# First pass of a two-layer encoder kernel: normalisation folded into the transposes, the conditioning row spread from eight columns, and a new order around the first strips

## The chip, the cores and the metric

The kernel runs on one core of one Trainium2 chip. The metric is device time in microseconds (us) for one execution of the whole kernel. The engines are named as the profile names them: PE (TensorE matmuls), PEld (its weight loads), DVE (VectorE), ACT (ScalarE), POOL (GpSimd) and SP (the queue that issues the DMAs).

## The reference, cut to what matters

A sequence of 1024 tokens of width 1024 goes through two layers, differential attention and latent attention, each with a modulated RMSNorm ahead of it. The changed part is the head of layer 0: the modulation from c, the normalised and modulated h, and the first projections of h.

```python
def _rmsnorm(x, g):
    y = xf * lax.rsqrt(jnp.mean(xf * xf, axis=-1, keepdims=True) + RMS_EPS)
    return (y * g).astype(x.dtype)

def _modulation(c, ada_w, ada_b):
    mod = jax.nn.silu(c) @ ada_w + ada_b
    shift, scale, gate = jnp.split(mod[:, None, :], 3, axis=-1)

for i in range(DEPTH):
    shift, scale, gate = _modulation(c, ada_w[i], ada_b[i])
    h = _rmsnorm(x, norm_g[i]) * (1.0 + scale) + shift
    ...            # layer 0: proj = h @ w_in0; q, k, v, z; differential attention; w_out0
    x = x + gate * y
return _rmsnorm(x, final_norm_g)
```

## The kernel before, in words

**Layout.** h is kept transposed: eight chunks k of 128 features by 512 tokens, for each half of the tokens. Every projection is summed over the eight chunks in PSUM. To keep f32 accuracy at the rate of the fp32r type, each operand is split into a high part (an fp32r cast on ACT) and a low part (the difference, on POOL or DVE), and each product is three matmuls: high by high, high by low, low by high.

**Modulation.** `mod_dot` (line 439) is one DVE instruction over 128x1024: it multiplies a block of `ada` weights, 128 output features by 1024, by silu(c) spread over all partitions, and sums along the row. A chunk needs two of them, shift into `modb` and scale into `moda`; line 447 then makes `moda` = (1 + scale) * norm_g. The spread row lies in the PSUM bank `cb`: c is loaded as one row (`crow`, line 565), goes through tanh on ACT and a product on DVE (lines 600 and 601), and two matmuls with a row of ones spread it (line 605).

**First half of the first pass** (lines 670 to 718, the loop over k from -1). For each chunk: two `ada` loads of 512 KB and a `w_v0` load, the two dots, four transposes of 128x128 of the x tiles into the bank `tr` (`h_chunk`, line 487), the two ACT readings of that bank (line 492 the high part, line 494 the f32 value), and on POOL the low part (line 497). x has been scaled by 1/rms before: the first 256 columns of each tile on ACT (lines 618 and 621), the rest on DVE (line 624, `x_rest`). Then PE sums four value tiles (`vacc`, lines 712, 713, 717) and the first key strip (`kacc`, lines 714, 715, 718), 15 matmuls of 128x512 for a chunk. Ahead of the pass PE runs matmuls of ones by ones (`keep_busy`, line 561; `WARM` gives their number before and after the spread of c).

**Between the halves.** The first query strip `wq0` is cast and split (line 218 on ACT, 219 on DVE), the x tiles of the second half are squared and scaled, `strip_half` sums the query strip for the first half in a bank of the tag `acc` (24 matmuls), and `store_v` (lines 377 and 378) evicts the four `vacc` banks.

**Second half of the first pass** (lines 739 to 755). The same chunks for the other 512 tokens, with 96 matmuls into four `vacc` banks; `tr` and a half of `cb` take the transposes in turn. Four dots of layer 1 (`mods_g`) stand between these chunks. After it come the second half of the key and query strips, and from there on a long run of matmuls to the end.

**Order.** The program text gives dependences; a scheduler at compile time orders the instructions on each engine. `tc.issue_after(ins)` puts what its block emits behind `ins` on the engine of `ins`. Buffers of a tag rotate: `ada` has four, `tr` one, `cb` one, `acc` two and `accx` three banks.

Of the kernel before, what the change touches and what calls it, by code (L numbers as in the profile page):

```python
# [11 lines left out]
F32 = mybir.dt.float32  # L12
# [9 lines left out]
P = 128  # L22
# [9 lines left out]
_W = [("norm_g0", KT), ("ada_bsh0", KT), ("ada_bsc0", KT), ("norm_g1", KT), ("ada_bsh1", KT),  # L32
      ("ada_bsc1", KT), ("subln_g", 1), ("q_a_norm_g", 3), ("kv_a_norm_g", 2), ("inv", 1), ("ada_bg0", KT), ("ada_bg1", KT)]
VEC, NVEC = {}, 0
# [27 lines left out]
X_ACT0 = (0, 2)  # L62
X_CUT = 256
WARM = (8, 9)
SIN_AT = (4, 5, 7)
# [16 lines left out]
def trunk(ctx: ExitStack, tc: tile.TileContext, A, out):  # L82
# [292 lines left out]
    def store_v(l, sp, acc, tt, fh, tag="vst", bufs=None):  # L375
        v = sp.tile([P, 2, HF], F32R, name="v_hl", tag=tag, bufs=bufs or VB[l])
        store_v.act = S.copy(v[:, 0, :], acc).ins
        V.tensor_sub(v[:, 1, :], acc, f32v(v[:, 0, :]))
# [62 lines left out]
    def mod_pair(l, j, ws, c_):  # L441

        g, bsh, bsc, a_, b_ = mods[l]
# [3 lines left out]
        return V.scalar_tensor_tensor(out=a_[:, js], in0=a_[:, js], scalar=1.0, in1=g[:, js], op0=ALU.add, op1=ALU.mult).ins  # L447

# [28 lines left out]

    def h_chunk(l, xn4, k, dst, hp, sub=G, wide=False, act=False, f32=None):

        _, _, _, a_, b_ = mods[l]  # L480
        if wide:
            tr = bank("cb", "trc", [P, D])[:, :HF].rearrange("p (j q) -> p j q", j=4)
        else:
            tr = bank("tr", "trh", [P, 4, P])
        for j in range(len(xn4)):
            nk = KT // len(xn4[j])
            PE.transpose(tr[:, j, :], xn4[j][k // nk][:, (k % nk) * P : (k % nk + 1) * P], ident)
# [4 lines left out]
        h_chunk.act = S.activation(hh, tr[:, :n, :], AF.Identity, bias=bk, scale=ak).ins  # L492
        if act:
            h_chunk.act = S.activation(tmp, tr[:, :n, :], AF.Identity, bias=bk, scale=ak).ins
        else:
            V.tensor_scalar(tmp, tr[:, :n, :], ak, bk, op0=ALU.mult, op1=ALU.add)
        return sub.tensor_sub(hl, tmp, f32v(hh)).ins
# [64 lines left out]

    crow = p1.tile([P, D], F32, name="crow", tag="ada", bufs=ADA_B)
    th = p1.tile([P, D], F32, name="cth", tag="ada", bufs=ADA_B)
    SP.dma_start(crow[0:1, :], A["c"])
    xs0 = [load_x(0, 0)]
# [32 lines left out]

    c_act = S.activation(th[0:1, :], crow[0:1, :], AF.Tanh, scale=0.5).ins  # L600
    c_last = V.scalar_tensor_tensor(out=crow[0:1, :], in0=th[0:1, :], scalar=1.0, in1=crow[0:1, :], op0=ALU.add, op1=ALU.mult).ins
    cb = bank("cb", "cb", [P, D])
    for f in range(2):
        fs = slice(f * HF, f * HF + HF)
# [5 lines left out]
    y0 = [None] * 4  # L610
    ss0 = sm.tile([P, 4], F32, name="xss")
# [4 lines left out]
    for j in range(3):  # L616
        y0[j] = y_[:, j : j + 1]
        S.mul(xs0[j][0][:, :X_CUT], xs0[j][0][:, :X_CUT], y0[j])
    sq_halves([xs0[3][0][:, :HF], xs0[3][0][:, HF:]], ss0[:, 3:4])
    y0[3] = inv_rms(ss0[:, 3:4], 1)[:, 0:1]  # L620
    h_chunk.act = S.mul(xs0[3][0][:, :X_CUT], xs0[3][0][:, :X_CUT], y0[3]).ins

    def x_rest(j):
        V.tensor_scalar(xs0[j][0][:, X_CUT:], xs0[j][0][:, X_CUT:], y0[j], None, op0=ALU.mult)

# [4 lines left out]
    def sines(n):  # L630
        with tc.issue_after(h_chunk.act):
            if n == 0:
                S.activation(kk, ang, AF.Sin, scale=0.5)
                S.activation(nsin, ang, AF.Sin, scale=-1.0)
            if n == 1:
                S.activation(ang, ang, AF.Sin)
                S.copy(c2, cb)
# [23 lines left out]
    for k in range(-1, KT + SKEW):  # L661
        if k + 1 < KT:
# [15 lines left out]
        if k < 0:  # L678
            with tc.issue_after(m_last):
                x_rest(0)  # L680
                x_rest(1)
        if k == 0:
            with tc.issue_after(m_last):
                x_rest(2)
                x_rest(3)
        if k == X1_AT:
            with tc.issue_after(mod_load.last):
                qraw = fetch_strip([A["w_s0"][0, 0, f] for f in range(2)], [4, 4])
            with tc.issue_after(fetch_strip.last):
                xs1 = [load_x(1, j) for j in range(4)]  # L690
            x_last = load_x.last
            with tc.issue_after(h_chunk.act):
                wq0 = split_strip(qraw, None, ada_pair)
            q_split = load_strip.last
        if 0 <= k < KT:
            h_chunk(0, xs0, k, h0[k][0], p1, act=True)
            if k % 4 == 0:
# [21 lines left out]
    ssa, ssb = [sm.tile([P, 2], F32, name="xss") for _ in range(2)]  # L719
    with tc.issue_after(m_last):  # L720
        for j in range(2):
            sq_piece(xs1[j][0], ssa[:, j : j + 1], False)
    with tc.issue_after(h_chunk.act):
        for j in range(2):
            sx = sm.tile([P, 1], F32, name="xs2")
            sq_piece(xs1[2 + j][0], ssb[:, j : j + 1], True)
            sq_piece(xs1[2 + j][1], sx, True)
            V.tensor_add(ssb[:, j : j + 1], ssb[:, j : j + 1], sx)
    norm_x(ssa, xs1[:2])
    yb = inv_rms(ssb, 2)  # L730
    for j in range(2):
        V.tensor_scalar(xs1[2 + j][0], xs1[2 + j][0], yb[:, j : j + 1], None, op0=ALU.mult)
        S.mul(xs1[2 + j][1], xs1[2 + j][1], yb[:, j : j + 1])
    load_tables()

    qacc = strip_half(wq0, h0, 0)
    q_mm = mm3.last
    for tt in range(4):
        store_v(0, p1b, vacc[tt], tt, 0)
    vacc = [bank("acc", "vacc") for _ in range(4)]  # L740
    for k in range(KT + SKEW1):
        if k < KT:
            if 0 < k <= MODS_K:
                next(mods_g)
            with tc.issue_after(q_split), tc.issue_after(q_mm):
                h_last = h_chunk(0, xs1, k, h0[k][1], p1, V if k in HL_V else G, k % 2 == 1)
        if k >= SKEW1:
# [69 lines left out]
    for h in range(NH):  # L817
        items += [(strip0(1, h), h0, k_done(h)), (strip0(0, h), h0, q_done(h)), (strip0(2, h), h0, z_done(h))]
    wv1 = [load_wv(A["w_v0"][k, 1], V) for k in range(WV1)]
    with tc.issue_after(mod_load.last):  # L820
        z0raw = fetch_strip([A["w_s0"][2, 0, f] for f in range(2)], [4, 4])
    with tc.issue_after(store_v.act):
        wv1 += [load_wv(A["w_v0"][k, 1], V) for k in range(WV1, KT)]
# [19 lines left out]
    for i in range(2):  # L843
        V.tensor_mul(lam4[:, 2 * i, :], lam4[:, 2 * i, :], lam4[:, 2 * i + 1, :])
        V.reduce_sum(lp[:, i : i + 1], lam4[:, 2 * i, :], axis=AX.X)
# [1586 lines left out]
def layout(inputs):  # L2432
# [40 lines left out]
    small["q_a_norm_g"] = cols(I["q_a_norm_g"], 3)  # L2473
    small["kv_a_norm_g"] = cols(I["kv_a_norm_g"], 2)
    small["inv"] = ca(np.tile(_ROPE_INV, 4).reshape(P, 1))
    w = I["w_in1"]
# [28 lines left out]
```

## Time and profile before

| | |
|---|---|
| median of 3 runs | 1382.29 us (1381.32 to 1382.38) |
| the profiled execution, its own time | 1382.89 us |
| its span | 1380.9 us |
| PE busy | 1361.0 us, 99% of the span |
| DVE, ACT, POOL busy | 949.2, 738.3, 708.7 us |
| first matmul of the first pass starts | 14.94 us |
| last matmul of the second half of the pass starts | 81.75 us |

Times inside the trace are counted from the start of the span. A busy PE is not PE at its peak: a matmul is shown with its latency (0.39 us for 128x512) though the next one starts sooner, so the spacing of the starts is read instead. The granted clock (PEclk) is the share of full TensorE speed.

### The profile page before, as it was taken

How to read it: one execution, taken by the hardware profiler on the slowest of the kernel's cores; microseconds unless marked ns; L12 is line 12 of the kernel's file. 1: busy time of each engine (PE TensorE's matmuls, PEld its weight loads, DVE VectorE, ACT ScalarE, POOL GpSimd, SP SyncE). 2: the span in 40 equal slices, each digit the busy share in tenths (PEclk: the TensorE clock that was granted, in tenths of full speed). 3: DMA queues.
4: the chain of work that ended last, by engine and by line, in shares of the span. 5: the costliest groups of instructions: out<-in, count | busy, mean ns of one | idle time of the engine just before them, and what ended most of it. 6: DMA issues, size and time to landing. Idle time of an engine off the chain costs nothing.

```text
span 1380.9 us, 20717 instructions
## 1 busy us (share of the span) xinstructions
PE 1361.0 (99%) x7322; PEld 1144.8 (83%) x7322; DVE 949.2 (69%) x1334; ACT 738.3 (53%) x1357; POOL 708.7 (51%) x556
## 2 busy tenths in 40 slices
PE   8999999999999999999999999999999999999997
PEld 6788888888888888887887887788888888888886
DVE  7764788877777767778597987645566555555584
ACT  5633465565655656566648543345454454455554
POOL 4425163647585757565695135532141373834673
PEclk8999999999999999999999999999999999999999
DMA  9867644353444444526654255599343463576373
GB/s 335 275 177 222 211 108 143 113 146 103 156 114 149 135 122 130 153 71 204 210 202 170 60 160 183 161 284 286 115 117 111 111 214 123 190 222 229 118 264 122
DMA packets 149386, 232.06 MB, mean 168 GB/s; under 512 B 20641, under 2 KB 57633, under 8 KB 149282
## 3 DMA queue, kind: packets, MB, share of 16 engines
q1 hardware_dynamic: 149138, 230.48, 53.4%
q8 instruction: 57, 0.93, 0.3%
q14 instruction: 47, 0.39, 0.1%
q10 hardware_dynamic: 144, 0.26, 0.1%
HBM read 144.74 MB, written 61.81 MB: 150 GB/s over the span
## 4 chain that ended last, share of the span: by engine, by line
PE 88%; DVE 4%; DMA 2%; ACT 2%; issue 1%; POOL 1%; SPq 0%; POOLq 0%; DVEq 0%; ACTq 0%
PE s L2109 10%; PE acc L173 9%; PE acc L175 9%; PE acc L174 9%; PE tr L398 8%; PE s L869 8%; PE pv L173 4%; PE pv L174 4%; PE pv L175 4%; PE oy L173 2%; PE oy L174 2%; PE oy L175 2%; PE vps L173 2%; PE vps L174 2%; PE vps L175 2%; PE zacc L175 1%
## 5 line engine op out<-in xcount | busy, mean ns | idle before, releaser
L400 ACT CAST pth<-tr 128x512 fp32r<-128x512 f32 x256 | 150.2, 587 | 279.2 <-PE tr L398 276.3
L401 DVE TENSOR_TENSOR ptl<-tr,pth 128x512 fp32r<-128x512 f32 x256 | 176.3, 689 | 144.6 <-ACT pth L400 143.9
L415 DVE TENSOR_REDUCE nm<-s 128x1 f32<-128x1024 f32 x192 | 234.0, 1219 | 53.7 <-PE s L869 42.9
L219 POOL TENSOR_TENSOR wl<-wraw,wh 128x512 fp32r<-128x512 f32 (+2 forms) x73 | 93.4, 1280 | 264.4 <-ACT wh L218 185.8
L417 ACT ACTIVATE e<-s,nm 128x1024 f32<-128x1024 f32 x128 | 143.7, 1122 | 35.0 <-DVE nm L415 34.4
L398 PE MATMUL tr<-ident,e 128*128 128x128 f32 x1024 | 154.8, 273 | 1.8 <-DVE ptl L401 1.5
L398 PEld LDWEIGHTS tr<-ident,e 128*128 128x128 f32 x1024 | 121.3, 140 | 42.5 <-DVE ptl L401 19.7
L173 PE MATMUL acc<-h0h,wh 128*128 128x512 f32 x360 | 149.5, 415 | 0.0
L173 PE MATMUL pv<-pth,vt 128*128 128x256 f32 x512 | 147.6, 288 | 0.0
L174 PE MATMUL pv<-ptl,vt 128*128 128x256 f32 x512 | 145.4, 284 | 0.0
L175 PE MATMUL pv<-pth,vt 128*128 128x256 f32 x512 | 144.6, 282 | 0.0
L175 PE MATMUL acc<-h0h,wl 128*128 128x512 f32 x360 | 142.0, 394 | 0.0
L174 PE MATMUL acc<-h0l,wh 128*128 128x512 f32 x360 | 141.4, 393 | 0.0
L174 PEld LDWEIGHTS pv<-ptl,vt 128*128 128x128 f32 x512 | 97.5, 190 | 2.5
L1203 POOL TENSOR_TENSOR wol<-wol,woh 128x512 fp32r<-128x512 f32 x56 | 81.9, 1486 | 34.0 <-ACT woh L1202 31.8
L173 PEld LDWEIGHTS pv<-pth,vt 128*128 128x128 f32 x512 | 97.2, 190 | 2.5
L175 PEld LDWEIGHTS pv<-pth,vt 128*128 128x128 f32 x512 | 97.4, 190 | 0.0
L869 PE MATMUL s<-ks,qa 128*128 128x512 f32 x256 | 82.7, 402 | 1.3 <-DVE e L877 1.2
L877 DVE SCALAR_TENSOR_TENSOR e<-s,z,e 128x1024 f32<-128x1024 f32 x64 | 82.2, 1284 | 2.2
L175 PEld LDWEIGHTS acc<-h0h,wl 128*128 128x128 f32 x360 | 67.6, 188 | 14.7
L869 PE MATMUL s<-ks,qb 128*128 128x512 f32 x256 | 79.6, 392 | 0.0
L174 PEld LDWEIGHTS acc<-h0l,wh 128*128 128x128 f32 x360 | 68.2, 189 | 9.2
(433 smaller groups left out, 3416.8 us busy)
## 6 DMA issues: line engine op xcount, KB each, us to landing
ada<-in_ada_ss SPq DMA_DIRECT2D x32, 512.0 KB, 6.1
vS<-v_hl SPq DMA_DIRECT2D x32, 512.0 KB, 5.5
vt<-vS SPq DMA_DIRECT2D x32, 512.0 KB, 4.6
wraw<-in_w_s SPq DMA_DIRECT2D x60, 256.0 KB, 2.8
wol<-tS SPq DMA_DIRECT2D x56, 256.0 KB, 5.3
tS<-ob SPq DMA_DIRECT2D x48, 256.0 KB, 2.2
rp_sw<-rp_raw SPq DMA_DIRECT2D x160, 64.0 KB, 2.0
bc_s<-bc_d SPq DMA_DIRECT2D x34, 256.0 KB, 4.0
```

The source lines that it names most:

```text
L173: PE.matmul(psum, ah, bh, start=first, stop=False, skip_group_check=skip)
L174: PE.matmul(psum, ah, bl, start=False, stop=False, skip_group_check=skip)
L175: mm3.last = PE.matmul(psum, al, bh, start=False, stop=last, skip_group_check=skip).ins
L219: sub = (V if pair_of else G).tensor_sub(l_[:, :n], raw[:, :n], f32v(h_[:, :n]))
L398: transpose_p.last = PE.transpose(tr[:, j, :], p[:, kt * P : (kt + 1) * P], ident).ins
L400: mk["S"] = S.copy(pth[kh][:, :, dst], tr).ins
L401: mk["V"] = V.tensor_sub(ptl[kh][:, :, dst], tr, f32v(pth[kh][:, :, dst])).ins
L415: mk["V"] = V.reduce_max(nm, s_ps, axis=AX.X, negate=True).ins
L417: mk["S"] = S.activation(e, s_ps, AF.Exp, bias=nm, scale=1.0, accum_out=zs).ins
L869: PE.matmul(s_ps[:, kc * HF : (kc + 1) * HF], src[:, c, ql], KS[h][kc][:, c, :], start=fst, stop=not fst)
L877: combined.append(V.scalar_tensor_tensor(out=e0, in0=e1, scalar=z1[:, 0:1], in1=e0, op0=ALU.mult, op1=ALU.add).ins)
L2109: PE.matmul(s_ps[:, kc * HF : (kc + 1) * HF], lhs, rhs(kc), start=i == 0, stop=i == 4)
```

## The change

What it does, part by part:

- `h_chunk` takes a diagonal matrix `dg`. In the first pass x is no longer scaled: the transpose by the identity becomes an ordinary f32 matmul of the x tile by diag(1/rms). `dg0` is built by four ACT products of 128x128, `dg1` (second half) by four on DVE. `x_rest` and the scaling of the second half's x go.
- c comes with the small vectors, as eight columns of 128. tanh and product run over 128x8; eight DVE products make diag(c_k), and eight f32 matmuls of ones by diag(c_k) spread it in `cb`.
- The matmuls of ones after the spread go from 9 to 15, and three more of them stand behind the first chunk's transposes (`KEEP0`).
- (1 + scale) * norm_g moves from DVE (line 447) to an ACT instruction of 128x1 (`mod_scale`).
- The copy of `cb` to `c2` and the casts of `wq0` move behind the last chunk of the first half on ACT. The first query strip is summed in the second half of the `cb` bank, and not in an `acc` bank.
- `store_v` of the first half is put behind the squares on ACT and the diagonals on DVE, the second half's ACT readings behind `store_v`; the four layer-1 dots go behind the last chunk; some casts of the later strips, the first `w_v0` casts for the other features (two early ones and not three) and the products for lambda are put behind named instructions.

```diff
-WARM = (8, 9)
+WARM = (8, 15)
+KEEP0 = 3
-    def strip_half(w, rhs, half):
+    def strip_half(w, rhs, half, acc=None):
-        acc = bank("acc", "acc")
+        acc = bank("acc", "acc") if acc is None else acc
...
-        mod_dot(ws[1], bsc[:, js], a_[:, js], c_)
-        return V.scalar_tensor_tensor(out=a_[:, js], in0=a_[:, js], scalar=1.0, in1=g[:, js], op0=ALU.add, op1=ALU.mult).ins
+        return mod_dot(ws[1], bsc[:, js], a_[:, js], c_).ins
+    def mod_scale(l, j):
+        S.activation(a_[:, js], a_[:, js], AF.Identity, bias=g[:, js], scale=g[:, js])
...
-            PE.transpose(tr[:, j, :], xn4[j][k // nk][:, ...], ident)
+            if dg is None:
+                PE.transpose(tr[:, j, :], piece, ident)
+            else:
+                h_chunk.tr = PE.matmul(tr[:, j, :], piece, dg[:, j, :], start=True, stop=True).ins
...
-    SP.dma_start(crow[0:1, :], A["c"])
-    c_act = S.activation(th[0:1, :], crow[0:1, :], AF.Tanh, scale=0.5).ins
-    c_last = V.scalar_tensor_tensor(out=crow[0:1, :], ...).ins
-        spread = PE.matmul(cb[:, fs], ones[0:1, :], crow[0:1, fs], start=True, stop=True).ins
+    c_act = S.activation(th, part("c"), AF.Tanh, scale=0.5).ins
+    V.scalar_tensor_tensor(out=cs, in0=th, scalar=1.0, in1=part("c"), op0=ALU.add, op1=ALU.mult)
+    for k in range(KT):
+        c_last = V.tensor_scalar(cd[:, k, :], ident, cs[:, k : k + 1], None, op0=ALU.mult).ins
+        spread = PE.matmul(cb[:, k * P : k * P + P], ones, cd[:, k, :], start=True, stop=True).ins
...
-        S.mul(xs0[j][0][:, :X_CUT], xs0[j][0][:, :X_CUT], y0[j])
+        diag(dg0[:, j, :], y_[:, j : j + 1])          # S.mul(dst, ident, y)
...
-                S.copy(c2, cb)                         # in sines(1)
-            with tc.issue_after(h_chunk.act):          # at k == X1_AT
-                wq0 = split_strip(qraw, None, ada_pair)
-            h_chunk(0, xs0, k, h0[k][0], p1, act=True)
+            mod_scale(0, k)
+            h_chunk(0, xs0, k, h0[k][0], p1, act=True, dg=dg0)
+            if k == 0:
+                with tc.issue_after(h_chunk.tr):
+                    for _ in range(KEEP0):
+                        PE.matmul(kacc[:, 0:P], ones, ones, start=True, stop=True)
...
+    with tc.issue_after(h_chunk.act):                  # after the first half's loop
+        S.copy(c2, cb)
+        wq0 = split_strip(qraw, None, ada_pair)
-    norm_x(ssa, xs1[:2])
-    ...                                                # scaling of xs1[2:] on DVE and ACT
+    diags(0, inv_rms(ssa, 2))
+    dg_last = diags(2, inv_rms(ssb, 2))
-    qacc = strip_half(wq0, h0, 0)
+    cbq = bank("cb", "cbq", [P, D])
+    qacc = strip_half(wq0, h0, 0, cbq[:, HF:])
+    turn += 1
     for tt in range(4):
-        store_v(0, p1b, vacc[tt], tt, 0)
+        with tc.issue_after(x_last), tc.issue_after(dg_last):
+            store_v(0, p1b, vacc[tt], tt, 0)
...
-            if 0 < k <= MODS_K:
-                next(mods_g)
-            with tc.issue_after(q_split), tc.issue_after(q_mm):
-                h_last = h_chunk(0, xs1, k, ..., k % 2 == 1)
+            with tc.issue_after(store_v.act), tc.issue_after(q_mm):
+                h_last = h_chunk(0, xs1, k, ..., cbq if k % 2 else None, dg=dg1)
+        if k == KT:
+            with tc.issue_after(h_chunk.v):
+                for _ in range(MODS_K):
+                    next(mods_g)
...
-    wv1 = [load_wv(A["w_v0"][k, 1], V) for k in range(WV1)]
+    with tc.issue_after(h_chunk.act):
+        wv1 = [load_wv(A["w_v0"][k, 1], V) for k in range(2)]
...
-    wz0 = split_strip(z0raw)
+    with tc.issue_after(store_v.act):
+        wz0 = split_strip(z0raw)
```

More of the change, by code (lines that the diff above doesn't have):

```diff
@@ L62 @@
 X_ACT0 = (0, 2)
-X_CUT = 256
-WARM = (8, 9)
+WARM = (8, 15)
+KEEP0 = 3
 SIN_AT = (4, 5, 7)
@@ L377, in store_v @@
         store_v.act = S.copy(v[:, 0, :], acc).ins
-        V.tensor_sub(v[:, 1, :], acc, f32v(v[:, 0, :]))
+        store_v.v = V.tensor_sub(v[:, 1, :], acc, f32v(v[:, 0, :])).ins
         th, tl = tt // 4, tt % 4
@@ L476, in norm_x, with h_chunk @@
                     V.tensor_scalar(piece, piece, y[:, j : j + 1], None, op0=ALU.mult)
-    def h_chunk(l, xn4, k, dst, hp, sub=G, wide=False, act=False, f32=None):
+    def h_chunk(l, xn4, k, dst, hp, sub=G, wide=None, act=False, f32=None, dg=None):
         _, _, _, a_, b_ = mods[l]
-        if wide:
-            tr = bank("cb", "trc", [P, D])[:, :HF].rearrange("p (j q) -> p j q", j=4)
+        if wide is not None:
+            tr = wide[:, :HF].rearrange("p (j q) -> p j q", j=4)
         else:
@@ L486, in h_chunk @@
             nk = KT // len(xn4[j])
-            PE.transpose(tr[:, j, :], xn4[j][k // nk][:, (k % nk) * P : (k % nk + 1) * P], ident)
+            piece = xn4[j][k // nk][:, (k % nk) * P : (k % nk + 1) * P]
+            if dg is None:
+                PE.transpose(tr[:, j, :], piece, ident)
+            else:
+                h_chunk.tr = PE.matmul(tr[:, j, :], piece, dg[:, j, :], start=True, stop=True).ins
         n = len(xn4)
@@ L561, in keep_busy @@
             PE.matmul(warm[:, 0:P], ones, ones, start=True, stop=True)
-    crow = p1.tile([P, D], F32, name="crow", tag="ada", bufs=ADA_B)
-    th = p1.tile([P, D], F32, name="cth", tag="ada", bufs=ADA_B)
-    SP.dma_start(crow[0:1, :], A["c"])
+    cd = p1.tile([P, KT, P], F32, name="cd", tag="ada", bufs=ADA_B)
+    th, cs = [sm.tile([P, KT], F32, name="cth") for _ in range(2)]
     xs0 = [load_x(0, 0)]
@@ L608, in trunk, with diag @@
     c2 = pg.tile([P, D], F32, name="c2")
-    y0 = [None] * 4
+    dg0 = p1.tile([P, 4, P], F32, name="dg", tag="dg", bufs=1)
+    def diag(dst, y):
+        return S.mul(dst, ident, y).ins
     ss0 = sm.tile([P, 4], F32, name="xss")
@@ L677, in trunk @@
                     next(angle_steps, None)
[L678 to L685, printed above, removed]
         if k == X1_AT:
@@ L718, in trunk, with diags @@
         PE.matmul(kacc, wk0[0][k0], hl, start=False, stop=k0 == KT - 1)
+    with tc.issue_after(h_chunk.act):
+        S.copy(c2, cb)
+        wq0 = split_strip(qraw, None, ada_pair)
     ssa, ssb = [sm.tile([P, 2], F32, name="xss") for _ in range(2)]
+    dg1 = p1.tile([P, 4, P], F32, name="dg", tag="dg", bufs=1)
+    def diags(j0, y):
+        for j in range(2):
+            ins = V.tensor_scalar(dg1[:, j0 + j, :], ident, y[:, j : j + 1], None, op0=ALU.mult).ins
+        return ins
     with tc.issue_after(m_last):
@@ L822, in trunk @@
     with tc.issue_after(store_v.act):
-        wv1 += [load_wv(A["w_v0"][k, 1], V) for k in range(WV1, KT)]
+        wv1 += [load_wv(A["w_v0"][k, 1], V) for k in range(2, KT)]
     with tc.issue_after(h_last):
@@ L2474, in layout @@
     small["kv_a_norm_g"] = cols(I["kv_a_norm_g"], 2)
+    small["c"] = cols(I["c"], KT)
     small["inv"] = ca(np.tile(_ROPE_INV, 4).reshape(P, 1))
```

30 lines of the change are left out of this document (11 added, 19 removed).

## The prediction

> **What bounds the kernel now.** I read the page first: the shares of the engines, the slices, the chain.
>
> ```profile
> PE 1361.0 (99%) x7322; PEld 1144.8 (83%) x7322; DVE 949.2 (69%) x1334; ACT 738.3 (53%) x1357; POOL 708.7 (51%) x556
> PEclk8999999999999999999999999999999999999999
> PE 88%; DVE 4%; DMA 2%; ACT 2%; issue 1%; POOL 1%; SPq 0%; POOLq 0%; DVEq 0%; ACTq 0%
> ```
>
> PE is busy for 99% of the span and carries 88% of the chain; its clock is below full only in the first slice of 34.5 us. So a change in the first 82 us moves the end by what it does to PE's own finishing of the first pass. Next I cut that pass into its stages and asked for the busy time of each.
>
> ```profile
> 14.94:21.50 6.56, 6.56 (x18) 5.29 (x19) 6.40 (x12) 3.25 (x6) 4.51 (x5) 0.54 1.01 374
> 21.50:49.35 27.85, 27.75 (x131) 21.84 (x129) 26.66 (x44) 17.36 (x28) 17.90 (x14) 1.00 0.92 321
> 49.35:57.24 7.89, 6.62 (x33) 5.36 (x33) 5.33 (x13) 6.28 (x16) 1.42 (x2) 1.00 0.79 202
> 57.24:82.38 25.14, 24.90 (x120) 20.30 (x121) 15.33 (x22) 8.47 (x13) 8.67 (x6) 1.00 0.67 210
> ```
>
> The columns are the stretch, its length, then PE, PEld, DVE, ACT and POOL, the granted clock, DMA share and GB/s. PE fills the first half after 21.5 us (27.75 of 27.85 us) and the second half (24.90 of 25.14); it has holes only between them, and it is slow in the first 6.5 us, where the clock is 0.54. DVE comes close behind PE in the first half (26.66), which a rival below uses.
>
> What PE is worth without holes follows from starts, not from busy time. In this list (start, duration, engine, line, operation) nine matmuls lie between the first two rows:
>
> ```profile
> 79.71 0.39 PE L175 MATMUL vacc<-wvh,h0l 128*128 128x512 f32 x1
> 81.75 0.39 PE L175 MATMUL vacc<-wvh,h0l 128*128 128x512 f32 x1
> 82.38 0.50 PE L173 MATMUL acc<-h0h,wq 128*128 128x512 f32 x1 [0.24 <-DVE v_hl L378]
> ```
>
> (81.75 - 79.71) / 9 = 0.227 us for one. The pass is 120 + 24 + 96 = 240 of them, 54.4 us. The transposes are priced below at 0.45 us a chunk; 15 chunks follow the first matmul, 6.7 us. That makes 61.1 us, but the pass runs from 14.94 to 81.98 us, 67.0 us. So 5.9 us are not work. Three are the clock:
>
> ```profile
> 10.78:14.20 3.42, 1.31 (x4) 0.55 (x4) 3.11 (x8) 2.31 (x6) 1.60 (x3) 1.00 1.04 405
> 14.20:17.61 3.41, 2.67 (x8) 2.28 (x9) 3.29 (x5) 2.38 (x4) 3.00 (x3) 0.50 1.04 407
> 17.61:21.02 3.41, 3.41 (x9) 2.64 (x8) 3.38 (x7) 1.13 (x2) 2.17 (x2) 0.50 1.03 360
> ```
>
> From 14.20 to 21.02 us the granted clock is 0.50, after a stretch in which PE had only four transposes. Work from 14.94 to 21.02 therefore took twice its time: 6.08 / 2 = 3.0 us lost. Of the rest, the waits of PE and of its weight loads between 14.9 and 60 us name 2.4:
>
> ```profile
> PE acc L173 <- DVE v_hl L378: 0.8, 1, 0.8
> PE vacc L173 <- ACT h0h L492: 0.4, 1, 0.4
> ...
> PEld trh L487 <- ACT h L494: 0.9, 2, 0.5
> PEld kacc L715 <- POOL wl L219: 0.3, 1, 0.3
> ```
>
> 5.9 us is thus all that any tidying of this pass can give, apart from an earlier start.
>
> **The change part by part.** First the diagonals, which run on the engine that bounds. The kernel has the same kind of matmul already, four f32 products of 128x128 near its end (line 926); it stands between the last two rows here, four transposes between the first two:
>
> ```profile
> 67.18 0.39 PE L175 MATMUL vacc<-wvh,h0l 128*128 128x512 f32 x1
> 68.08 0.40 PE L174 MATMUL vacc<-wvl,h0h 128*128 128x512 f32 x1
> 1304.52 0.39 PE L175 MATMUL oy<-woh,oal 128*128 128x512 f32 x1
> 1304.75 1.05 PE L926 MATMUL rb<-dg,ones 128*128 128x128 f32 x8
> 1305.87 0.40 PE L174 MATMUL oy<-wol,oah 128*128 128x512 f32 x1
> ```
>
> Both pairs of rows hold two 128x512 spacings beside the four small ones: 0.90 - 0.45 = 0.45 us for four transposes, 1.35 - 0.45 = 0.90 us for four f32 matmuls (each is two instructions, x8). So a chunk costs 0.45 us more, and 15 chunks cost 15 x 0.45 = **+6.75 us** (the first chunk's lie ahead of the first matmul). Bounds: 6.3 by a spacing of 0.107 us for an instruction, 3.6 if the first half hides its seven (the second rival). I take the full price, since PE fills both halves.
>
> The Trainium skill, "TensorE: Matmul & The Clock Gate", in its section Terms, calls transpose mode 4x faster for FP32. The rows show twice (0.90 to 0.45 us), and the measurement decides; by the page the diagonals would cost 15 x 3 x 0.45 = 20 us in all.
>
> The clock. New matmuls of ones (15 for 9) and the eight spreading matmuls fill PE from about 4.4 to 9.5 us; diagonals and the three matmuls behind the first chunk's fill part of 11.5 to 14.5. If the clock stays up the gain is **-3.0**, if nothing changes 0. The stretch with only 1.31 us of transposes lost the clock, a fully busy one regained it. The new stretch has some 0.9 + 0.6 us of ordinary matmuls, and its forerunner a hole of 1.3 us. I take **-2.7**: even a clock that falls at 14.2 has a full stretch behind it and comes back one stretch earlier.
>
> On this the same page (Part 1 and Part 4) says that the window is about 3.4 us, free-running, and that transposes don't count as activity. The steps of 3.41 us agree, and so does the loss at 14.20 after transposes alone; by it ordinary matmuls as transposes help, which is the value taken.
>
> The start. Its chain, in the timeline:
>
> ```profile
> 1.18 0.33 SPq L565 DMA_DIRECT2D crow<-in_c  x1
> 1.56 1.78 SPq L523 DMA_DIRECT2D xt<-in_x  x4
> 11.29 1.28 DVE L439 CUSTOM_DVE_ANT_0 ada<-ada,cb,vec 128x1024 f32<-128x1024 f32 x1 [0.24 <-DMA ada<-in_ada_ss]
> 13.85 0.16 DVE L447 SCALAR_TENSOR_TENSOR moda<-moda,vec 128x1 f32<-128x1 f32 x1
> 14.11 0.78 ACT L492 ACTIVATE h0h<-trh,modb,moda 128x512 fp32r<-128x512 f32 x1 [0.23 <-DVE moda L447]
> 14.94 0.80 PE L712 MATMUL vacc<-wvh,h0h 128*128 128x512 f32 x1 [1.18 <-ACT h0h L492]
> ```
>
> The first dot waits for its `ada` block, then two dots, line 447, h0h, matmul. The c load goes from SP's queue, so x and `ada` are issued 1.56 - 1.18 = 0.38 us sooner; against it `mod_scale` on ACT takes 0.2 us (the nearest row is 0.206 us for 128x4, below) where DVE took 0.16, and one more hand-over. The x side is ready before: ACT builds a diagonal in 0.39 us where it scaled 256 columns in 0.50. **-0.3**, between -0.5 and +0.5. The spreading (eight DVE products of 128x128, at most the 0.39 us of ACT's, so 3.1 us, each followed by a matmul of 0.90 / 4 = 0.23 us) starts once the small vectors are there and lies under the loads of x and `ada`, whose wait ends at 11.29; without that cover it would cost its 3.3 us.
>
> ```profile
> L925 ACT ACTIVATE dg<-ident,zz x4: 390/397/405, 1290.1 to 1292.0; 128x128 f32<-128x128 f32 x4
> L952 ACT ACTIVATE sl_w<-zz x16: 205/206/212, 172.8 to 664.6; 128x4 f32<-128x4 f32 x16
> L447 DVE SCALAR_TENSOR_TENSOR moda<-moda,vec 128x1 f32<-128x1 f32 x8 | 4.1, 507 | 0.3
> L624 DVE TENSOR_SCALAR xt<-xt,rq_y 128x768 f32<-128x768 f32 x4 | 3.5, 883 | 0.0
> L618 ACT ACTIVATE xt<-xt,rq_y 128x256 f32<-128x256 f32 x3 | 1.3, 499 | 1.0 <-POOL rq_y L169 1.0
> L637 ACT COPY c<-cb 128x1024 f32<-128x1024 f32 x1 | 1.0, 1016 | 0.0
> L378 DVE TENSOR_TENSOR v_hl<-vacc,v_hl 128x512 fp32r<-128x512 f32 x4 | 2.7, 685 | 1.0 <-ACT v_hl L377 1.0
> 17.27 1.27 POOL L219 TENSOR_TENSOR wl<-wraw,wh 128x512 fp32r<-128x512 f32 x1
> ```
>
> The first half's own holes. A chunk will be 15 x 0.227 + 0.90 = 4.3 us of PE, where DVE needs two dots, 2.7 us, and sheds 3.5 (line 624) and 4.1 us (line 447); ACT gains eight of 0.2 and loses the copy of `cb`. The 0.9 + 0.3 us of waits go: **-1.2**. But at full clock the first chunk catches up with POOL, which makes the value's low part, h's low part and then the key strip's (till 18.54 us): 14.65 + 8 x 0.227 + 0.9 + 0.23 = 17.6, so some **+0.5** new wait (0 to 1.5).
>
> Between the halves. The query strip no longer waits for an evicted bank: **-0.8** (0 to -1.0). What is late next is `wq0`: its casts now queue on ACT behind the last chunk and the 1.0 us copy. The last chunk's transposes stand ahead of two chunks' matmuls, 6.8 us before the first half's end; two readings (0.78 each), the copy and two casts of 0.6 leave some 3 us, the difference on DVE 2. The evictions now wait behind the squares; who waits for them is the second half's `vacc` banks. PE has 24 x 0.227 + 1.8 = 7.2 us before it needs these; squares and four differences of 0.685 take an estimated 5. The second half's entry had 0.4 us of wait; two chunks' diagonals (1.8 us) now cover ACT's 0.78: **-0.3** (-0.4 to +1). The x scaling that leaves DVE and ACT here was off PE's path: 0.
>
> What is moved: the four layer-1 dots and their four loads on SP were late already (PE does not wait for them), the z strip's loads queue behind those loads and are needed only after the query strip, over 10 us later: 0, and if that cover went, up to a dot, 1.3 us. The lambda products and the casts put behind evictions: 0 on the same ground. The 0.24 us before 82.38 stays, within -0.4 to +0.5.
>
> Sum: 6.75 - 2.7 - 0.3 - 1.2 + 0.5 - 0.8 - 0.3 = **+1.95 us** on the profiled execution's 1382.89, which stands 0.6 above the median. On the median of 1382.29 that is **1384.2**. All terms at their best ends give 6.3 - 3.0 - 0.5 - 1.2 - 1.0 - 0.4 - 0.4 = -0.2.
>
> **The rivals.**
>
> The clock stays down (slower). If the clock falls during the wait for the first dots and isn't back before about 20 us, the 2.7 go back: 1.95 + 2.7 = +4.65, 1386.9. It decides from 0.8 us, 1.6 us of half clock. For it speaks the trace: a stretch with 2.67 us of PE work (14.20 to 17.61) didn't bring the clock back. Against it: some of that were transposes.
>
> The first half hides its diagonals (no change, a little faster). If loads and dots pace it, seven chunks' 0.45 don't count: 1.95 - 3.15 = -1.2, 1381.1. For it DVE's 26.66 of 27.85 us and loads at 321 GB/s; against it PE's 27.75 and DVE's lighter load.
>
> The later order changes (faster). PE's waits after 82 us are small; the largest in total:
>
> ```profile
> PE zacc L175 <- POOL wl L219: 1.9, 3, 0.7
> PE tr L398 <- DVE ptl L401: 1.5, 4, 0.6
> PE s L869 <- DVE e L877: 1.2, 3, 0.6
> ```
>
> They make 4.6 us together. A new order could close them; to be faster by 0.2% it must give 1.95 + 2.76 = 4.7: 1379.5 at most. Nothing in the diff reaches these places.
>
> The f32 matmul costs four transposes: 20 us for 6.75, +15, 1397.6. The row of line 926 speaks against it. The page named above says so; hence a rival.
>
> **How the numbers follow.** About 0.2% (2.8 us) is what a measurement of this kernel can tell from no change. Forecast 0.59, clock 0.18, hidden 0.12, later order 0.10, four transposes 0.01. The forecast's own range goes from the best ends, 1382.1, to 1386.0, where the start and the first chunk's wait stand at their upper ends (+0.8 and +1.0). Taking in the clock rival and the hidden one with 0.8 us around each gives 1380.4 to 1387.8, which leaves the other two and some tail outside. Faster: 0.10, the later order. Slower: 0.18 + 0.01 and 0.06 of the forecast's upper end, 0.25. No change: 0.53 + 0.12 = 0.65.
>
> **What would show it.** In the profile after: four diagonals between two 128x512 matmuls spaced 1.35 us and not 0.90; the granted clock at 1.00 from 14.2 on (or from 17.6, the forecast's lower case); first matmul at about 14.6; the query strip right behind `kacc`; the last `vacc` matmul of the second half at 83 to 84 us and not 81.75. I am wrong if the first pass ends before 81 us, which needs a much earlier start or hidden diagonals, or if time is lost or won after it.

## The result, and the profile after

The changed kernel takes 1389.07 us (median of 6 executions, 1388.03 to 1391.67), the kernel before 1382.05 us beside it (6 executions, 1380.67 to 1382.38). The ratio is 1.0055, 95% interval 1.0042 to 1.0068: the change costs 7.0 us, where the forecast said 1.95 and its range ended at 1387.8. The profiled execution of after took 1388.03 us (span 1386.2), the shortest of its six; that of before was 0.8 us above its median. So the two traces differ by 5.1 us, not by 7.0.

The page of after, in the lines that were shown of before:

```profile
PE 1370.5 (99%) x7416; PEld 1153.6 (83%) x7416; DVE 946.9 (68%) x1330; ACT 738.8 (53%) x1363; POOL 707.9 (51%) x556
PEclk9999999999999999999999999999999999999999
PE 88%; DVE 3%; DMA 2%; ACT 2%; issue 1%; POOL 1%; SPq 1%; POOLq 0%; ACTq 0%; DVEq 0%
```

PE still bounds, and the first slice of the clock is now full. The four stages of the pass, cut at the same events as before (first `vacc` matmul, 21.5 us, end of the first half, first `vacc` matmul of the second half, first matmul behind the pass):

```profile
13.97:21.50 7.53, 7.50 (x40) 6.09 (x41) 7.46 (x11) 4.59 (x8) 6.36 (x6) 1.00 1.04 402
21.50:48.21 26.71, 26.71 (x138) 22.59 (x137) 23.46 (x36) 20.64 (x38) 15.79 (x14) 1.00 0.97 346
48.21:56.99 8.78, 7.55 (x42) 6.26 (x40) 3.70 (x11) 3.36 (x9) 1.37 (x2) 1.00 0.98 256
56.99:84.85 27.86, 27.75 (x144) 23.41 (x145) 15.46 (x22) 7.97 (x12) 10.33 (x7) 1.00 0.48 152
```

The granted clock is 1.00 throughout, and PE has no hole left in the first half. Holes of 1.2 us stay in the third stage, and the second half grew from 25.1 to 27.9 us. The starts that the forecast named, from the timeline of after (start, duration, engine, line, operation):

```profile
10.19 1.28 DVE L439 CUSTOM_DVE_ANT_0 ada<-ada,cb,vec 128x1024 f32<-128x1024 f32 x1 [0.24 <-DMA ada<-in_ada_ss]
12.72 0.39 ACT L452 ACTIVATE moda<-moda,vec 128x1 f32<-128x1 f32 x1
13.97 0.50 PE L712 MATMUL vacc<-wvh,h0h 128*128 128x512 f32 x1 [0.91 <-ACT h0h L501]
18.51 0.40 PE L718 MATMUL kacc<-h0l,wh 128*128 128x512 f32 x1
19.87 0.39 PE L713 MATMUL vacc<-wvl,h0h 128*128 128x512 f32 x1
47.98 0.40 PE L718 MATMUL kacc<-h0l,wh 128*128 128x512 f32 x1
48.22 0.39 PE L173 MATMUL cbq<-h0h,wq 128*128 128x512 f32 x1
84.62 0.39 PE L175 MATMUL vacc<-wvh,h0l 128*128 128x512 f32 x1
84.85 0.39 PE L173 MATMUL acc<-h0h,wh 128*128 128x512 f32 x1
1310.44 1.05 PE L942 MATMUL rb<-dg,ones 128*128 128x128 f32 x8
```

From 18.51 to 19.87 run two 128x512 matmuls and four diagonals: 1.36 us, 1.35 as priced. The query strip follows `kacc` at the next slot. The first matmul behind the pass starts at 84.85 (before 82.38): +2.47 us. The last row is line 926 of before under its new number; from the end of the pass to it the changed kernel needs 1310.44 - 84.85 = 1225.6 us, before 1304.75 - 82.38 = 1222.4. **So of the 5.3 us between the spans 2.5 were lost in the pass and 3.2 behind it, where the forecast had 0** (0.4 came back near the end).

The place where the pass lost what was not forecast, the entry of the second half, in the timeline of after:

```profile
52.40 5.18 SPq L380 DMA_DIRECT2D vS<-v_hl  x3
53.58 0.39 PE L175 MATMUL cbq<-h0h,wq 128*128 128x512 f32 x1
55.15 0.61 PE L496 MATMUL cbq<-dg,xth 128*128 128x128 f32 x4
55.67 0.58 ACT L377 CAST v_hl<-vacc 128x512 fp32r<-128x512 f32 x1 [5.42 <-DMA vS<-v_hl]
56.15 0.78 ACT L501 ACTIVATE h0h<-trh,modb,moda 128x512 fp32r<-128x512 f32 x1
56.99 0.50 PE L173 MATMUL vacc<-wvh,h0h 128*128 128x512 f32 x1 [1.23 <-ACT h0h L501]
```

ACT stands still for 5.42 us ahead of the fourth eviction's cast, until a DMA `vS<-v_hl` has landed: `v_hl` has three buffers here, and the fourth cast needs the first one back. The change put the ACT readings of the second half behind that cast, so `h0h` starts at 56.15 though its transposes were there before; PE waits 1.23 us.

### The profile page after: what moved, and what is told of

Read it like the earlier page. It is cut to its first block, busy times and chain, and to the rows that moved or that the text cites. A ratio compares the mean times of both kernels' runs of the same rounds, so it can differ in the third digit from the quotient of the medians.

```text
span 1386.2 us, 20928 instructions
## 1 busy us (share of the span) xinstructions
PE 1370.5 (99%) x7416; PEld 1153.6 (83%) x7416; DVE 946.9 (68%) x1330; ACT 738.8 (53%) x1363; POOL 707.9 (51%) x556
## 4 chain that ended last, share of the span: by engine, by line
PE 88%; DVE 3%; DMA 2%; ACT 2%; issue 1%; POOL 1%; SPq 1%; POOLq 0%; ACTq 0%; DVEq 0%
PE s L2125 10%; PE acc L173 9%; PE acc L175 9%; PE acc L174 9%; PE tr L398 8%; PE s L885 8%; PE pv L173 4%; PE pv L175 4%; PE pv L174 4%; PE oy L173 2%; PE oy L175 2%; PE oy L174 2%; PE vps L173 2%; PE vps L175 2%; PE vps L174 2%; PE zacc L175 2%
## 5 line engine op out<-in xcount | busy, mean ns | idle before, releaser
L1219 POOL TENSOR_TENSOR wol<-wol,woh 128x512 fp32r<-128x512 f32 x56 | 81.5, 1480 | 33.7 <-ACT woh L1218 32.2
L344 POOL TENSOR_TENSOR rp_sw<-rp_sw,sinT 128x512 f32<-128x512 f32 x40 | 52.6, 1315 | 52.1 <-DMA rp_sw<-rp_raw 51.8
```

## The experiments

Two theories stood after the comparison: (1) the entry waits for the fourth `v_hl` buffer; (2) the loss behind the pass is one of addresses. The matmuls there have no more waits than before, they only follow each other more slowly. In the compiled program the new `c` columns (32 bytes per partition) and the new tile `cth` (four buffers of 32 bytes) move the large buffers that are laid out behind them from the low end of SBUF by 160 bytes; those laid out from the high end stay. The rival of (2) is that the changed pass leaves a different order or state behind. The order did change there: the key strip's second half now runs ahead of the query strip's (`acc<-h0h,wh` at 84.85, where before has `acc<-h0h,wq` at 82.38), and on DVE, ACT and POOL a few instructions stand elsewhere, up to 142 us. From there on the order on every engine is that of before.

**Before, moved by 32 and by 160 bytes.** The kernel has a pad at its low end; nothing else is touched, and the order on every engine is that of before.

```diff
-PADL = 96 // 4
+PADL = 128 // 4     # b_pad32; 256 // 4 in b_pad160
```

> The kernel before with nothing changed but the pad ahead of the left side of SBUF, 128 bytes a partition and not 96: every buffer of the left side moves by 32 bytes, the order on each engine stays. Theory addresses (the changed kernel moves the same buffers by 160 bytes, an odd multiple of 32, and lost 2.8 us after the first pass): +2.5 us, about 1384.5, and against the kernel before the starts of like matmuls drift by some 2.4 us between 140 and 700 us. Rival order (the later loss comes from the new order and times after the first pass): 0, within 0.5 us.

> The kernel before with a pad of 256 bytes and not 96, so that every large buffer of the left side after the first pass stands where the changed kernel has it (160 bytes on); same order. Theory addresses: a steady lag grows behind the first pass to some 3.5 us, less waits that close, +2.8 us in all, 1384.4. Rival order: 0.

Measured: 32 bytes 1383.60 us (11 executions, ratio 1.0013, 1.0004 to 1.0022), 160 bytes 1385.26 us (11, ratio 1.0021, 1.0012 to 1.0030). Moving the buffers alone makes the unchanged kernel slower. From the end of the pass to line 926 the kernel moved by 160 bytes takes 1225.9 us, 3.6 more than before's 1222.4:

```profile
81.75 0.50 PE L173 MATMUL acc<-h0h,wq 128*128 128x512 f32 x1 [0.57 <-DVE v_hl L378]
1307.69 1.05 PE L926 MATMUL rb<-dg,ones 128*128 128x128 f32 x8
```

Of the 3.6 us 1.4 come in one step between 104 and 140 us, where PE waits 1.1 us for `v_hl`; a second execution of before has a step of 1.0 us there too (below). Of the rest 1.1 grow steadily from 140 to 400 us. The busy time of the engines between 140 and 400 us shows in what way; first before, then before moved by 160 bytes, then after (columns: stretch, length, then PE, PEld, DVE, ACT, POOL with the number of instructions, clock, DMA share, GB/s):

```profile
140.00:400.00 260.00, 259.43 (x1438) 221.39 (x1437) 202.37 (x285) 150.91 (x278) 137.90 (x110) 1.00 0.46 133
```

```profile
140.00:400.00 260.00, 259.45 (x1432) 220.25 (x1431) 201.74 (x283) 148.93 (x274) 136.15 (x109) 1.00 0.46 133
```

```profile
140.00:400.00 260.00, 259.45 (x1431) 220.31 (x1430) 199.75 (x280) 148.63 (x274) 134.25 (x107) 1.00 0.44 131
```

PE is as busy in all three, at full clock, with 6 or 7 instructions fewer in the moved ones, about 0.45%. A busy share can't show such a loss; only counts and starts do. The mean spacing of 128x512 matmuls between 140 and 480 us is 230.1 ns in before and 231.6 ns in after; from 104 to 135 us, where DVE is busy for about half of the time and not for 78%, it is 226.7 or 226.8 ns in every kernel of this study.

**After, moved by 32 more.** The shift becomes 192 bytes, a multiple of 64.

```diff
-PADL = 96 // 4
+PADL = 128 // 4
```

> The changed kernel with the pad at 128 bytes and not 96: its left-side buffers stand 192 bytes, three times 64, from where the kernel before has them, and not 160; same order. Theory addresses: the 2.8 us behind the first pass go, 1389.1 - 2.6 = 1386.5, and the lag behind the kernel before stays near 2.5 us from 100 us to the end. Rival order: 1389, and the lag grows to 5 us by 700 us as in the changed kernel.

Measured: 1389.06 us (5, ratio 1.0046, 1.0034 to 1.0059), a miss. The spacing did improve a little (230.6 ns), and from the end of the pass to line 942 it needs 1224.7 us, 0.9 less than after; but it is not back at 1222.4, so a multiple of 64 is not the rule. That profile also lost 1.5 us in the pass: PE's wait at the entry was nearly the same (1.4 us), but here the granted clock fell behind it. This bears on the median: the four of its five executions with a mean clock of 0.997 took 1388.88 to 1389.17 us, the one with 0.999 took 1386.65, near the 1386.5 expected. One execution can't settle it. The stretch from 58 to 61 us, first this kernel, then after:

```profile
58.00:61.00 3.00, 3.00 (x17) 3.00 (x17) 2.45 (x5) 0.78 (x1) 0.00 (x0) 0.56 0.97 227
```

```profile
58.00:61.00 3.00, 3.00 (x22) 2.78 (x23) 2.86 (x5) 1.56 (x2) 0.27 (x1) 1.00 0.96 257
```

**The fourth eviction from another tag.** The fourth `v_hl` takes a buffer that is free. The order changes a little with it (on ACT the fourth cast now stands ahead of the copy of `kacc`, and a few instructions near 58 us and up to 87 us change places); behind the pass it is that of after.

```diff
-            store_v(0, p1b, vacc[tt], tt, 0)
+            store_v(0, *((p1b, vacc[tt], tt, 0) if tt < 3 else (p1, vacc[tt], tt, 0, "xt", 6)))
```

> The changed kernel with the fourth eviction of the first half written to a buffer of another tag (xt) and not to one of the three v_hl buffers, so that its cast on ACT needn't wait for the first one's DMA to land. Theory buffer (the second half's first reading on ACT stands behind that cast): the 1.2 us wait of PE at 57 us goes and the second half starts some 1.4 us sooner, 1389.1 - 1.5 = 1387.6. Rival (the entry waits for the diagonals themselves or for the evicted banks): the wait stays under another name, 1389.

Measured: 1386.85 us (5, ratio 1.0035, 1.0021 to 1.0048), 2.2 less than after. Its timeline:

```profile
55.75 0.78 ACT L501 ACTIVATE h0h<-trh,modb,moda 128x512 fp32r<-128x512 f32 x1 [4.34 <-PE trh L496]
56.59 0.50 PE L173 MATMUL vacc<-wvh,h0h 128*128 128x512 f32 x1
```

`h0h` now waits for PE's own products and PE for nothing. The start of this execution was 0.8 us later (first matmul at 14.79), so the gain at the entry is more than the 0.4 us between 56.99 and 56.59: from the end of the first half (48.83, after 47.98) it is 7.76 us and not 9.01.

**The same with the second half scaled and transposed as before.**

```diff
-    diags(0, inv_rms(ssa, 2))
-    dg_last = diags(2, inv_rms(ssb, 2))
+    norm_x(ssa, xs1[:2])
+    ...                       # scaling of xs1[2:] on DVE and ACT, as before
-                h_last = h_chunk(0, xs1, k, ..., cbq if k % 2 else None, dg=dg1)
+                h_last = h_chunk(0, xs1, k, ..., cbq if k % 2 else None)
```

> As a_v4, and in the second half x is scaled on DVE and ACT and transposed by the identity again, as in the kernel before; the first half keeps its diagonals. Theory price (an f32 matmul costs PE 0.45 us a chunk more than a transpose, and PE bounds): 8 x 0.45 = 3.6 us below a_v4, 1384.0. Rival hidden (the second half waits for ACT, DVE or POOL anyway): as a_v4 within 1 us, 1387.

Measured: 1384.56 us (11, ratio 1.0023, 1.0014 to 1.0032), 2.3 less. The second half of this kernel:

```profile
55.53:80.35 24.82, 24.82 (x121) 20.41 (x122) 15.61 (x23) 7.98 (x12) 8.67 (x6) 1.00 0.67 205
```

24.8 us against 27.5 with diagonals (56.59 to 84.07 in the kernel above): 2.7 us for six chunks, 0.45 each. In the second half the diagonals are paid in full.

**The addresses of before in the changed kernel.** The tanh tile goes to a pool where it moves nothing, and the pad is 32 bytes smaller, which makes up for the eight columns of `c`: a first kernel with the fourth eviction mended, a second with nothing else changed. The order on every engine stays.

```diff
-PADL = 96 // 4
+PADL = 64 // 4
-    th, cs = [sm.tile([P, KT], F32, name="cth") for _ in range(2)]
+    th, cs = [p1.tile([P, KT], F32, name="cth", tag="cth", bufs=2) for _ in range(2)]
```

> As a_v4 (the fourth eviction with a buffer of its own), and the large left-side buffers after the first pass at the addresses of the kernel before: the two small tiles of c lie in the first pass's pool and the pad is 64 bytes and not 96. Same order as a_v4. Theory addresses: the steady growth of the lag behind the kernel before (3.5 us in a_v4) goes, the lag stays near 1.8 us; 1386.85 - 2.8 = 1384.0. Rival order: 1386.9.

> The changed kernel with the addresses alone restored (the tanh tile in another pool, the pad 128 bytes smaller; the order on every engine is the same as the changed kernel's). Addresses theory: 3.2 us less than the changed kernel, 1385.9, as in the pair of kernels with the fourth eviction's buffer mended; the pass still ends at 84.6 us with its entry wait of 1.2 us, and the lag behind before stays at +2.5 to +3 us from 107 us to the end. Rival (the drift belongs to the order of the later work, and the other pair's gain is by chance): 1388 to 1389, with the lag growing to +5 us again.

Measured: with the eviction mended 1383.65 us (11, ratio 1.0014, 1.0005 to 1.0023), 3.2 less than without this edit. Alone 1387.12 us (5, ratio 1.0040, 1.0026 to 1.0053), 2.0 less than after and 1.2 more than expected. The addresses theory holds for the work behind the pass; the rival falls, since the changed order is still there. The rows of the second kernel, from two views:

```profile
140.00:400.00 260.00, 259.45 (x1435) 221.26 (x1435) 200.52 (x281) 148.06 (x272) 133.39 (x107) 1.00 0.47 135
58.00:61.00 3.00, 2.88 (x13) 2.45 (x13) 2.52 (x4) 0.80 (x2) 0.00 (x0) 0.64 0.95 261
```

```profile
56.49 0.59 ACT L377 CAST v_hl<-vacc 128x512 fp32r<-128x512 f32 x1 [5.53 <-DMA vS<-v_hl]
57.81 0.50 PE L173 MATMUL vacc<-wvh,h0h 128*128 128x512 f32 x1 [2.27 <-ACT h0h L501]
87.24 0.39 PE L173 MATMUL acc<-h0h,wh 128*128 128x512 f32 x1
1309.50 1.05 PE L942 MATMUL rb<-dg,ones 128*128 128x128 f32 x8
```

Behind the pass the count is back at 1435 and line 942 comes 1222.3 us after the pass, as in before (1222.4); with the eviction mended it is 1221.9. What is missing of the 3.2 us went ahead of it: the DMA that the fourth eviction needs landed later, PE waited 2.27 us and not 1.23, and the granted clock fell to half for one stretch of 3.4 us (0.64 in the mean from 58 to 61 us). The pass ends 2.4 us later than in after, at 87.24.

**Transposes in both halves.** The kernel with the eviction and the addresses mended, and x scaled and transposed by the identity in the first half too; matmuls of ones, query strip and orders stay.

```diff
-            h_chunk(0, xs0, k, h0[k][0], p1, act=True, dg=dg0)
+            h_chunk(0, xs0, k, h0[k][0], p1, act=True)
+                x_rest(0)     # and the others, as before
```

> As a_v4_addr, and both halves scale x and transpose by the identity, as the kernel before; the spread of c from eight columns, the matmuls of ones (15, and 3 behind the first chunk), the query strip in the cb bank and the new order stay. Theory price: 15 x 0.45 = 6.75 us below a_v4_addr, about 1377.3, faster than both kernels. Rival clock (only ordinary matmuls as transposes keep the clock up): the granted clock falls to 0.5 for one or two steps of 3.4 us in the first half and 1.7 to 3 us come back, about 1379.7.

Measured: 1389.15 us (6, ratio 1.0046, 1.0033 to 1.0060): a miss by 12 us, lost in three places. The first half did not gain the 3 us: it ends at 47.99 us, against 48.12 with diagonals. PE's waits in it and behind the pass (two views, columns: us in total, times, longest):

```profile
PE trh L495 <- DVE xt L633: 1.2, 1, 1.2
PE trh L495 <- ACT h L504: 0.7, 2, 0.5
PE vacc L722 <- ACT h0h L502: 0.6, 1, 0.6
PE kacc L725 <- POOL wl L220: 0.3, 1, 0.3
```

```profile
PE vps L174 <- DVE v_hl L379: 1.8, 1, 1.8
PE s L891 <- DVE e L899: 1.8, 3, 0.8
PE s L891 <- DMA qb<-qb: 1.1, 1, 1.1
```

With the scaling back on DVE (line 633) PE waits for it, and for the dots that stand behind it on DVE: from `kacc` to `kacc` the second and third chunk take 5.77 and 4.64 us where the later ones take 3.87, which gives 2.7 of the 3.15 us back. The second place is the entry of the second half. On ACT the squares of x stand behind the copy of `kacc` in this program and start at 48.90 us, where they started at 46.08 in the kernel with transposes in the second half alone; PE waits 2.3 us for `h0h`, and the clock fell there (0.58 from 57.1 to 61 us). End of the first half to end of the pass takes 35.5 us, against 32.2 in that kernel. The third is behind the pass: from its end (83.50) to line 948 (1311.76) this program takes 1228.3 us, 6 more than the kernel without this edit, in steps between 104 and 140 and between 400 and 600 us. Its order there differs from that kernel's; on DVE, ACT and POOL it is nearly before's (a cast of `wvh` and the eviction of one `v_hl` stand elsewhere). The named waits don't explain it all: before's other execution has the first (0.7 us), the kernel without this edit has the third (0.5), and why they are longer here no run shows.

**Before once more.** The unchanged program in another execution, to see how far two traces of one program drift apart, and what of the forecast's clock is typical.

> The kernel before once more, to see how far two traces of one program drift apart. Theory addresses: the starts of like matmuls from 100 us on stay within 0.5 us of the first trace of it. Rival (the drift is between executions, not between programs): they wander by 1 us or more, as between the kernel before and the changed one.

Measured: 1381.94 us, span 1379.9. The rival's drift is there: from 100 us on the starts lie between 0.97 us ahead of the first trace's and 0.51 us behind them. It comes in steps (1.0 us between 104 and 140 us, where PE waits 0.7 us for `v_hl`) that mostly close again: from the end of the pass to line 926 it takes 1222.6 us, 0.2 more than in the first trace. So differences of 1 us inside a trace show nothing; the steady loss does. Between 140 and 400 us the starts of like matmuls fall behind those of the first trace by 0.06 us here and by 0.03 and 0.10 in the two kernels with the addresses put back, by 1.09 to 1.18 in the five moved by 32 or 160 bytes, by 0.54 in the one moved by 192, and by 0.35 in the one with transposes in both halves.

The clock is 1.00 where the forecast's trace had 0.50. Two stretches there, and the landmarks:

```profile
13.60:17.00 3.40, 2.47 (x12) 1.86 (x13) 3.22 (x5) 2.28 (x4) 3.40 (x3) 1.00 1.03 402
17.00:20.40 3.40, 2.65 (x11) 1.56 (x10) 3.37 (x7) 1.24 (x2) 2.04 (x2) 1.00 1.03 405
```

```profile
14.23 0.50 PE L712 MATMUL vacc<-wvh,h0h 128*128 128x512 f32 x1 [0.90 <-ACT h0h L492]
47.84 0.39 PE L718 MATMUL kacc<-h0l,wh 128*128 128x512 f32 x1
81.44 0.50 PE L173 MATMUL acc<-h0h,wq 128*128 128x512 f32 x1 [0.31 <-DVE v_hl L378]
```

The same program at full clock starts 0.7 us sooner, ends its first half 1.1 us sooner (47.84 for 48.96) and the pass 0.9. At full clock PE has more room between the matmuls (2.65 of 3.40 us busy), since it comes to wait for the other engines (from the second chunk on 0.5 us for `h0h`, 0.6 for low parts from POOL, 0.2 for ACT's readings of the transposes): the 3.0 us of the cold clock had mostly been spent in holes that are there anyway. Of the 59 executions of before timed beside the experiments, the 17 with a mean granted clock of 0.995 have a median of 1382.0 us and the 8 with 0.999 one of 1381.5.

**All three costs taken out.**

> All three suspected costs taken out of the changed kernel at once: the fourth eviction's buffer from another tag, the second half scaled and transposed as before, and the 160 bytes of shift undone. What stays of the change: diagonals in the first half, c from eight columns, the matmuls of ones, the query strip in the bank of cb, the order of the casts. If the three costs are separate they add: taken from 1389.1 the entry's 2.2, the diagonals' 2.3 and the addresses' 3.2 give 1381.4, no different from before (1381.6), and the matmuls after the pass keep before's pace (lag behind before constant within 0.3 us from 140 us on, apart from steps). If the first half's seven diagonals (3.2 us) were paid on PE and not hidden, the pass would end 3 us later than the 80.1 us of the kernel with two of these edits, and the time would be about 1384.5. If the addresses' price depends on what else is changed, it stays near the 1384.6 of the kernel without this edit.

Measured: 1382.58 us (11, 1379.91 to 1383.43; before 1381.98 on the same chip), ratio 1.0003 (0.9994 to 1.0012): no different from before. Its pass and its stretch:

```profile
79.68 0.39 PE L173 MATMUL acc<-h0h,wh 128*128 128x512 f32 x1
1302.54 1.05 PE L938 MATMUL rb<-dg,ones 128*128 128x128 f32 x8
```

```profile
140.00:400.00 260.00, 259.43 (x1440) 221.10 (x1438) 202.36 (x285) 152.94 (x281) 140.31 (x112) 1.00 0.44 131
```

The pass ends 1.8 us sooner than in before's better execution (81.44), and the way to line 938 is 1222.9 us. The profiled execution was the shortest of the eleven; what the median loses against it, 2.7 us, no trace shows, so it stays open whether the remaining half of the change is worth something.

By the ratios the steps from after to here are 1.0055, 1.0035 (eviction mended), 1.0023 (second half by transposes), 1.0003 (addresses): 2.8, 1.7 and 2.8 us of 1382. Each ratio is known to 1.2 to 1.8 us either way, so a single step is known to some 2 us only; what carries the first two are the traces (1.25 us at the entry, 2.7 us in the second half). Together the three make up the 7 us.

## Why the prediction was wrong, point by point

The forecast failed in two steps, and two of its terms were sized on one execution.

1. **What is behind the pass (0), measured +3.2 us.** The forecast looked there for waits and for a new order, and wrote "Nothing in the diff reaches these places". No new waits came, rightly; the order did change up to 142 us, but it costs nothing (1222.3 us with the addresses put back, 1222.4 in before). The forecast did not count what the new tiles do to the addresses of the others. The rows before and after the 160-byte move carry this: 1438 and 1432 PE instructions in the same 260 us, with no other edit. It is shown in both directions: moved in the unchanged kernel, and moved back in three pairs of kernels (1225.6 to 1222.3 us, 1224.9 to 1221.9, 1225.4 to 1222.9). That "time is lost or won after it" was among the forecast's own signs of being wrong.
2. **The second half's entry (-0.3, bounds -0.4 to +1), measured +0.8 in the profile (wait 0.4 to 1.23), 2.2 us in the medians of the kernels with and without it.** The step says of the evictions that "who waits for them is the second half's `vacc` banks". On ACT the readings of `h` stand behind them too, and the fourth cast waits for a buffer and so for a DMA's landing. The forecast gave the price of the queue's instructions, not of the wait of the last one in it. The traces account for 1.25 of the 2.2 us (7.76 for 9.01); the rest is inside the medians' uncertainty.
3. **The clock (-2.7).** It did stay at 1.00, as forecast; the gain is not there in the medians, since a full clock in the first half runs into holes (before again: 1.1 us at the end of the first half, 0.7 of them from the start; the half itself takes 33.6 us warm and 34.0 cold, so 0.4 and not 2.7 in it). The term counted as gain what at full clock becomes waiting.
4. **The diagonals (+6.75).** The price of 0.45 us a chunk is right in both halves. In the second half it is paid (2.7 us for six chunks; two more stand at the entry). In the first half PE does it (4.34 us from `kacc` to `kacc`, no hole left), but transposes in their place end at the same time: the rival that the first half hides its diagonals was right about the place, and the work that hides them is the scaling on DVE that the diagonals take away.
5. **The first half's sum** was right by luck, by errors that cancel: 3.15 - 2.7 - 1.2 + 0.5 = -0.25 forecast, from the first matmul to the last of `kacc`; measured 34.01 us against 34.02. By the spacings (119 of 0.227 us and seven chunks of 0.45 or 0.90) the work is 30.2 us with transposes and 33.3 with diagonals. So before had 3.4 us of holes at full clock (33.6) and after has 0.7: the diagonals' 3.15 us filled holes of which the forecast had counted 1.2 us as waits and the rest as the cold clock.
6. **The start (-0.3)**: -0.97 between the two traces, -0.26 against before's other execution. Within it `mod_scale` took 0.39 us and not the 0.2 of the nearest row.
7. **The query strip (-0.8)**: from the last `kacc` matmul to the strip's first 1.23 us became 0.24, so -1.0. The hole behind the pass shrank by 0.4, the lower bound of what was said of it.

Summed over the pass, the terms gave +1.95 and the traces show +2.47; the last `vacc` matmul, forecast at 83 to 84 us, came out at 84.62. The rest between the two traces is the addresses. Of the rivals, the clock staying down did not happen at its place, but the clock fell at the entry of the second half in three kernels of the experiments. The later order did change in after, and neither gained nor lost time. The f32 matmul at four transposes did not happen (0.9 us for four diagonals).

## What to carry to other kernels

Where PE is busy for 99% and a change adds or resizes a tile, put the large buffers back where they were (a pad is enough) before judging the change: the move alone was worth 2 to 4 us of 1382 here. When work is bound behind an eviction, follow the eviction's own destination buffer to the DMA that frees it. A gain read from one execution's cold clock or from a hole is to be looked for in a second execution first: a faster clock and a filled hole may be the same microseconds.

## What the runs showed of the hardware that was not expected

- **Addresses.** The spacing of the 128x512 matmuls between 140 and 480 us depends on where buffers lie: 230.0 to 230.2 ns at before's addresses (before twice and four others), 231.6 to 231.8 ns 160 bytes further (four kernels), 231.4 at 32, 230.6 at 192. From 104 to 135 us, where DVE and ACT are less busy, it is 226.7 or 226.8 ns in all; that their work makes the difference is not shown. The Trainium skill, "SBUF — State Buffer", section Door 1, describes lines of 16 bytes. All these moves are whole lines, so by that alone they would change nothing, and the counts above say otherwise. Which buffer meets which, and by what rule, was not tried.
- **The clock at short waits.** Waits of PE of 1.23 and 1.43 us at the same place left the clock at 1.00 in after and at 0.56 (58 to 61 us) in the changed kernel moved by 32 more bytes; with 2.27 us, in the kernel with the addresses alone put back, it was 0.64. In the 3.41 us ahead of the fall PE was busy for 1.87 and 1.03 us in these two kernels; in after, in the 3.41 us from 54.42 that hold its wait, for 2.07 us. The Trainium skill, "TensorE: Matmul & The Clock Gate", in Why this matters for your kernels, warns of idle gaps above some 3 us. Here 1.43 and 2.27 us were enough, half and three quarters of that. Part 1 of that page of the Trainium skill calls the window free-running. The traces agree in that the fall is not tied to the wait: it came 1.4 and 1.0 us behind the end of the wait in these two kernels, and 0.1 us ahead of it in the one with transposes in both halves.
- An ACT instruction of 128x1 whose bias and scale are both read from columns took 0.39 us, where 128x4 without them took 0.21.
